# Down weights in longer runs, eight slots and another order of tiles, in a kernel that ends in 16 experts

## The chip, the cores and the metric

The kernel runs on one core of a Trainium2 chip. The metric is the time of one execution on the device in microseconds (us), a median over runs. Lower is better.

## What is computed

The program is three transformer layers over 256 tokens of width 1024, in float32. The first two have a mixer (a recurrence, two kinds of attention), a cross attention and a gated feed-forward part; the third has an adaptive modulation, a windowed attention with a gated branch, and a feed-forward part of 16 experts. Each expert takes the 32 tokens that score highest for it (cap = 2 x 256 / 16). The change is about the experts:

```
aff = softmax(h @ w_router);  gates, idx = top_k(aff.T, cap)      # 16 experts, 32 tokens each
xs  = h[idx]
hid = silu(xs @ w_gate[e]) * (xs @ w_up[e])     # w_gate, w_up: 16 x 1024 x 2816
out = (hid @ w_down[e]) * gates                 # w_down: 16 x 2816 x 1024
y   = zeros.at[idx].add(out);   x = x + gate2 * rms_norm(y)
```

The weights of one expert are 3 x 1024 x 2816 x 4 bytes = 34.60 MB (11.53 MB each of gate, up and down), those of all experts 553.6 MB. Each is read once.

## The kernel before

The first part of the program (mixers, cross attentions, feed-forward parts and the third layer up to its routing) runs out of a pool of tiles called `work`, whose first lines give every tag its place: the split activations `hH` and `hL`, `raw` (three weight buffers of 1 MB that SyncE fills), `wh` and `wl` (the weights split in two halves by ScalarE and VectorE), `gain`, `xg`, `dg`, `junk`, `mH` and `mL`, and small ones. `run_program` issues the loads of `raw` as buffers come free. The routing's constants and `mods` lie in another pool at the upper end.

`routing` ends that part: it norms the tokens, scores them, finds the 32 best per expert with VectorE, builds the selectors `sel` and gathers the tokens by matmul out of `mH` and `mL` into `xsT` (L1588 to L1594).

`experts` then frees `work` and takes the same memory for `e_pool`. `SLOTS_AT` is the order of its tiles in memory: a number is a slot for weights (5632 columns, 22,528 bytes a partition), a name is another tile. There are `E_BUFS` slots, used in turn. `loads` lists all pieces in their order: per expert four times a gate and an up piece (256 rows, two per partition, so that a partition's 22,528 bytes are contiguous in memory, and the piece is one block of 2.88 MB), then six down pieces. A down piece is two blocks of 256 rows (two rows per partition, 8192 bytes contiguous, 2 MB in all), the sixth one block. `feed` issues pieces on SyncE's queue (L1641 down, L1644 gate and up) as far as slots go; `take` feeds one more whenever TensorE's code comes to a piece. A piece waits for everything that used the memory of its slot: the first seven for tiles of `work` and of the routing, all later ones for the matmuls on the slot's piece before. SyncE issues in order, so one that waits holds back those behind it.

Per expert, TensorE multiplies the 32 tokens (`xsT`, 32 columns) by gate and up pieces (L1670): seven matmuls per 128 rows and kind, four of 512 and three of 256 columns, each into its 32 partitions of `pg` and `pu`. ScalarE and VectorE make `hid` of them (L1675 to L1677), TensorE turns it by six transposes, ScalarE and VectorE copy the result to `hT` (L1684, L1688). Then come the down matmuls (L1698) into `pd`, ScalarE's copies to `ds` (L1700, L1701), four matmuls with the gates' selector `sT` into `po` (L1705), which put the 32 tokens in their places, and VectorE's additions to `y` in SBUF (L1710). At the end `y` is normed (squares on ScalarE, L1717; the gain on VectorE, L1718; the root on GpSimd, L1722 and L1723), added to `x` and stored.

## Time and profile before

| | us |
|---|---|
| median of three runs | 2364.9 (2364.6 to 2369.95) |
| the profiled execution | 2368.78 |
| its span | 2367.0 |
| first matmul of the experts | 1085.83 |
| last matmul record's start of the down weights, and its length | 2347.58, 5.32 |

A page shows one profiled execution: busy times of the engines, the span in 40 slices (59.2 us each) with the share of the 16 DMA engines and the bytes that they moved, and the chain of waits that ended last. The table of stretches gives the same for any stretch: busy time of each engine, the granted clock of TensorE as a share of 2.4 GHz, the mean busy share of the DMA engines (a little over 1 where transfers overlap) and GB/s. A timeline lists instructions in order of time: start, length, engine, line, operation, tiles, and in brackets the idle time before it and what ended that.

### The profile page before, as it was taken

What the parts mean: (1) busy time and instruction counts of PE and PEld (TensorE: products, weight loads), DVE (VectorE), ACT (ScalarE), POOL (GpSimd) and SP (SyncE); (2) the same over time, 40 slices, a digit from 0 to 9 for tenths busy, and PEclk for the clock granted to TensorE, in tenths of its full rate; (3) what the DMA queues carried; (4) which work ended last, traced back from release to release, by engine and by line L of the source; (5) the groups of instructions that cost most, each with busy time, mean ns of one, the idle gap of its engine ahead of it and who ended that gap; (6) DMA issues with size and microseconds to landing.
All of it is one profiled execution on the core that took longest, in us unless ns stands there. A gap on an engine that the chain in (4) does not pass through costs nothing.

```text
span 2367.0 us, 29153 instructions
## 1 busy us (share of the span) xinstructions
PE 1844.4 (78%) x12660; PEld 1169.9 (49%) x12660; DVE 743.7 (31%) x1099; ACT 539.7 (23%) x866; POOL 54.4 (2%) x96
## 2 busy tenths in 40 slices
PE   7999999999989999987666666665666656666665
PEld 7889899989878888973111111111111111111211
DVE  5775555567656555652000000000000000000001
ACT  4554444445534333531000000000000000000000
POOL 0010000000000000010000000000000000000000
PEclk9999999999999999978888778888778897887788
DMA  7345465553559886539999999999999999999996
GB/s 219 125 147 183 160 195 179 161 155 127 195 178 301 281 279 195 203 154 384 428 428 425 423 429 425 425 425 428 425 425 427 428 424 423 429 426 424 425 428 282
DMA packets 202320, 747.06 MB, mean 316 GB/s; under 512 B 17712, under 2 KB 148416, under 8 KB 163408
## 3 DMA queue, kind: packets, MB, share of 16 engines
q1 hardware_dynamic: 199600, 744.39, 80.0%
q8 instruction: 99, 1.62, 0.3%
q10 hardware_dynamic: 2592, 0.81, 0.2%
q14 instruction: 29, 0.24, 0.0%
HBM read 743.99 MB, written 1.05 MB: 315 GB/s over the span
## 4 chain that ended last, share of the span: by engine, by line
DMA 50%; PE 40%; DVE 5%; ACT 2%; POOL 1%; issue 1%; SPq 0%; ACTq 0%; POOLq 0%; DVEq 0%
DMA ed<-in_w_down_dram 23%; DMA eu<-in_w_up_dram 22%; DMA eg<-in_w_gate_dram 4%; PE pu L1670 3%; PE pd L1698 2%; PE fu L249 2%; PE fu L251 2%; PE fu L250 2%; PE fg L249 2%; PE fg L251 2%; PE fg L250 2%; PE facc L251 2%; PE facc L250 2%; PE facc L249 2%; DVE wl L207 1%
## 5 line engine op out<-in xcount | busy, mean ns | idle before, releaser
L1670 PE MATMUL pu<-eu,xsT 128*32 128x512 f32 (+1 forms) x1792 | 274.8, 728 | 180.7 <-DMA eu<-in_w_up_dram 180.7
L207 DVE TENSOR_TENSOR wl<-raw,wh 128x1024 fp32r<-128x1024 f32 (+1 forms) x284 | 341.6, 1216 | 226.7 <-ACT wh L206 226.1
L1698 PE MATMUL pd<-ed,hT 128*32 128x512 f32 x1408 | 230.3, 742 | 146.9 <-DMA ed<-in_w_down_dram 143.4
L206 ACT CAST wh<-raw 128x1024 fp32r<-128x1024 f32 (+1 forms) x284 | 292.2, 1043 | 224.5 <-PE fg L250 44.1
L1670 PE MATMUL pg<-eg,xsT 128*32 128x512 f32 (+1 forms) x1792 | 235.0, 636 | 112.7 <-DMA eg<-in_w_gate_dram 112.7
L1670 PEld LDWEIGHTS pu<-eu,xsT 128*32 128x32 f32 x1792 | 78.6, 143 | 370.9 <-DMA eu<-in_w_up_dram 214.4
L1676 DVE SCALAR_TENSOR_TENSOR hid<-hid,pg 128x512 f32<-128x512 f32 (+1 forms) x32 | 17.6, 549 | 693.2 <-ACT hid L1675 693.2
L1670 PEld LDWEIGHTS pg<-eg,xsT 128*32 128x32 f32 x1792 | 71.2, 129 | 282.2 <-DMA eg<-in_w_gate_dram 152.9
L1698 PEld LDWEIGHTS pd<-ed,hT 128*32 128x32 f32 x1408 | 48.7, 125 | 316.3 <-DMA ed<-in_w_down_dram 171.8
L1675 ACT ACTIVATE hid<-pg 128x512 f32<-128x512 f32 (+1 forms) x32 | 15.6, 489 | 755.8 <-PE pg L1670 743.7
L1710 DVE TENSOR_TENSOR y<-y,po 128x512 f32<-128x512 f32 x60 | 41.2, 687 | 374.3 <-PE po L1705 374.3
L249 PE MATMUL fu<-hH,wh 128*128 128x256 f32 x352 | 100.4, 285 | 0.0
L251 PE MATMUL fu<-hH,wl 128*128 128x256 f32 x352 | 100.3, 285 | 0.0
L250 PE MATMUL fu<-hL,wh 128*128 128x256 f32 x352 | 100.2, 285 | 0.0
L249 PE MATMUL fg<-hH,wh 128*128 128x256 f32 x352 | 99.6, 283 | 0.0
L250 PE MATMUL fg<-hL,wh 128*128 128x256 f32 x352 | 99.5, 283 | 0.0
L251 PE MATMUL fg<-hH,wl 128*128 128x256 f32 x352 | 99.5, 283 | 0.0
L1700 ACT COPY ds<-pd 128x512 f32<-128x512 f32 x16 | 9.4, 586 | 362.0 <-PE pd L1698 362.0
L251 PE MATMUL facc<-wh,dL 128*128 128x512 f32 x176 | 69.3, 393 | 0.0
L250 PE MATMUL facc<-wl,dH 128*128 128x512 f32 x176 | 68.9, 391 | 0.0
L249 PE MATMUL facc<-wh,dH 128*128 128x512 f32 x176 | 68.6, 390 | 0.0
L250 PEld LDWEIGHTS fu<-hL,wh 128*128 128x128 f32 x352 | 67.9, 193 | 0.0
(566 smaller groups left out, 3208.9 us busy)
## 6 DMA issues: line engine op xcount, KB each, us to landing
eg<-in_w_gate_dram SPq DMA_DIRECT2D x64, 2816.0 KB, 36.4
eu<-in_w_up_dram SPq DMA_DIRECT2D x64, 2816.0 KB, 37.3
ed<-in_w_down_dram SPq DMA_DIRECT2D x80, 2048.0 KB, 37.5
raw<-in_w_in_dram SPq DMA_DIRECT2D x31, 1024.0 KB, 5.6
adw<-in_w_ada_dram SPq DMA_DIRECT2D x24, 1024.0 KB, 8.5
raw<-in_w_gate_dram SPq DMA_DIRECT2D x22, 1024.0 KB, 5.4
raw<-in_w_up_dram SPq DMA_DIRECT2D x22, 1024.0 KB, 5.2
raw<-in_w_down_dram SPq DMA_DIRECT2D x22, 1024.0 KB, 4.9
```

The source lines that it names most:

```text
L206: nc.scalar.copy(h, v)
L207: nc.vector.tensor_tensor(l, v, h.bitcast(F32), op=OP.subtract)
L249: nc.tensor.matmul(o, aH, bH, start=first, stop=False)
L250: nc.tensor.matmul(o, aH, bL, start=False, stop=False)
L251: nc.tensor.matmul(o, aL, bH, start=False, stop=last)
L1670: nc.tensor.matmul(o, B["xsT"][:, k, 32 * e:32 * e + 32], w[:, a, d, :], start=k == 0, stop=k == KC - 1)
L1675: nc.scalar.activation(d, g, AF.Tanh, scale=0.5)
L1676: nc.vector.scalar_tensor_tensor(d, d, 1.0, g, op0=OP.add, op1=OP.mult)
L1698: nc.tensor.matmul(pd[n][32 * j:32 * j + 32, :], hT[:, 2 * (d // 4) + c % 2, s:s + 32], w[:, (c % 4) * D + n * 512:(c % 4) * D + n * 512 + ...
L1700: nc.scalar.copy(ds_[:, :512], pd[0])
L1710: nc.vector.tensor_tensor(yb, yb, po, op=OP.add)
```

## The change

Down weights come in four pieces per expert, each 22,528 contiguous bytes per partition: partition p holds rows 22p to 22p + 21 (90,112 bytes), and piece i is the i-th quarter of that. A piece is five and a half rows, 11 half rows of 512 columns. The last piece of all is cut in three (3072, 1536 and 1024 columns). So every expert has 12 pieces of 2.88 MB where it had eight of 2.88 MB and six of 2 or 1 MB.

So that the rows 22p + j lie on partition p, the features of `hid` are taken by quarters of 704: quarter q on partitions 32q and on, in 512 columns (`pg`, `pu`) and 192 more (`pr`, one PSUM bank for both kinds), eight matmuls per 128 rows and kind. VectorE's 32x32 transpose over `hid`, read with a step of 22, makes `hT` in one instruction. The second half of `pd` shares the bank of `pr`.

The experts' sums stay in four PSUM banks `y00` to `y11` over all experts. At the end they are squared out of PSUM, and the gain goes to a tile `yg` in a weight slot. The sum of squares is added on VectorE. `rows16` of the routing has a tile of its own. The space kept for DMA descriptors in SBUF is set to 512 bytes, the tags of `work` stand in another order with three gaps, and there are eight slots in the order of `SLOTS_AT`.

```
-E_BUFS = 7
-SLOTS_AT = [1, 5, 3, 4, 6, "y", "hid", "hT", "ds", "sT", "fs", 0, 2]
+E_BUFS = 8
+SLOTS_AT = [1, 2, 4, 5, 6, 7, 0, 3, "hid", "hT", "ds", "sT", "fs"]
...
+    tile_(work, (P, 48), "gap0")
     hH = tile_(work, (P, KC, S), "hH", F32R)
     hL = tile_(work, (P, KC, S), "hL", F32R)
-    for tag, n, dt, bufs in (("gain", D, F32, 2), ("dg", P, F32, 2), ("raw", 2048, F32, RAW_BUFS), ("wh", 1024, F32R, HALVES), ("wl", 1024, F32R, HALVES),
-                             ("junk", D, BF16, 1), ("tiny1", 1, F32, 8), ("xg", D, F32, 3), ("tiny8", 8, F32, 6), ("tiny2", 2, F32, 6), ("tiny16", 16, F32, 2),
-                             ("mH", 2048, F32, 1), ("mL", 2048, F32, 1)):
+    tile_(work, (P, 16), "gap1")
+    for tag, n, dt, bufs in (("raw", 2048, F32, RAW_BUFS), ("wh", 1024, F32R, HALVES), ("wl", 1024, F32R, HALVES), ("gap2", 320, F32, 1),
+                             ("gain", D, F32, 2), ("dg", P, F32, 2), ("xg", D, F32, 3), ("junk", D, BF16, 1), ("mH", 2048, F32, 1), ("mL", 2048, F32, 1),
+                             ("tiny1", 1, F32, 8), ("tiny8", 8, F32, 6), ("tiny2", 2, F32, 6), ("tiny16", 16, F32, 2)):
...
-        sc = work.tile([16, 512], F32, name="rows16", tag="junk", bufs=1)
+        sc = tile_(p, (16, 512), "rows16")
...
-                    nw = min(2, NW - 2 * k)
-                    to = t[:, :nw * 2 * D].rearrange("p (d c n) -> p d c n", d=nw, c=2)
-                    src = I["w_down_2"][0, e, 512 * k:512 * k + 256 * nw, :].rearrange("(d p c) n -> p d c n", p=P, c=2)
-                    if st["n"] == len(loads) - 1:
-                        for n0 in range(0, D, 512):
-                            nc.sync.dma_start(to[:, 0, :, n0:n0 + 512], src[:, 0, :, n0:n0 + 512])
-                    else:
-                        nc.sync.dma_start(to.rearrange("p d c n -> p d (c n)"), src.rearrange("p d c n -> p d (c n)"))
+                    src = I["w_down_2"][0, e].rearrange("(p j) n -> p (j n)", p=P)[:, 2 * D_FF * k:2 * D_FF * (k + 1)]
+                    cut = (0, 3072, 4608, 2 * D_FF) if st["n"] == len(loads) - 1 else (0, 2 * D_FF)
+                    for c0, c1 in zip(cut, cut[1:]):
+                        nc.sync.dma_start(t[:, c0:c1], src[:, c0:c1])
...
-                        for b in range(2):
-                            for j in range(4 - b):
-                                d = slice(j, j + 5, 4) if b == 0 else slice(j + 8, j + 9)
-                                o = pg[n][32 * j:32 * j + 32, b, :512 - 256 * b].rearrange("p (d f) -> p d f", f=256)
-                                nc.tensor.matmul(o, B["xsT"][:, k, 32 * e:32 * e + 32], w[:, a, d, :], start=k == 0, stop=k == KC - 1)
+                        xs = B["xsT"][:, k, 32 * e:32 * e + 32]
+                        for q in range(4):
+                            nc.tensor.matmul(pg[n][32 * q:32 * q + 32, :], xs, w[:, a, q, 0:512], start=k == 0, stop=k == KC - 1)
+                        for q in range(4):
+                            nc.tensor.matmul(rest[n][32 * q:32 * q + 32, :], xs, w[:, a, q, 512:], start=k == 0 and n == "g", stop=k == KC - 1 and n == "u")
...
-            hT = e_pool.tile([P, 6, P], F32, name=f"hT{e}", tag="hT", bufs=1)
-            hv = hid.rearrange("p d (q a) -> p d a q", a=2)
-            pt = pq.tile([P, 4, P], F32, name=f"pt{e}a", tag="pm", bufs=2)
-            for m in range(4):
-                nc.tensor.transpose(pt[:, m, :], hv[:, m // 2, m % 2, :], ident)
-            nc.scalar.copy(hT[:, 0:4, :], pt)
...
+            hT = e_pool.tile([P, NJ, 32], F32, name=f"hT{e}", tag="hT", bufs=1)
+            nc.vector.transpose(hT, hid.rearrange("p (a j) -> p j a", j=NJ))
...
-            for q in range((NW + 1) // 2):
-                w = take("d", e, q)
+            for i in range(4):
+                w = take("d", e, i)
                 for n in range(2):
-                    for c in range(4 * q, min(4 * q + 4, 2 * NW)):
-                        d, j = c // 2, c % 4
-                        s = 32 * (d % 4)
-                        nc.tensor.matmul(pd[n][32 * j:32 * j + 32, :], hT[:, 2 * (d // 4) + c % 2, s:s + 32], ...
+                    for h in range(11 * i, 11 * i + 11):
+                        j = h // 2
+                        if h % 2 == n:
+                            nc.tensor.matmul(pd[n][32 * (j % 4):32 * (j % 4) + 32, :], hT[:, j, :], w[:, 512 * (h - 11 * i):512 * (h - 11 * i) + 512], start=j < 4, stop=j + 4 >= NJ)
             nc.scalar.copy(ds_[:, :512], pd[0])
-            nc.scalar.copy(ds_[:, 512:], pd[1])
+            if e < NE - 1:
+                nc.scalar.copy(ds_[:, 512:], pd[1])
+            else:
+                nc.vector.tensor_copy(ds_[:, 512:], pd[1])
             for n in range(2):
                 for t in range(2):
-                    po = pq.tile([P, 512], F32, name=f"po{e}_{t}{n}", tag="pm", bufs=2)
-                    nc.tensor.matmul(po, sT[:, t * P:(t + 1) * P], ds_[:, n * 512:(n + 1) * 512], start=True, stop=True)
...
-                        nc.vector.tensor_tensor(yb, yb, po, op=OP.add)
+                    nc.tensor.matmul(y[t][n], sT[:, t * P:(t + 1) * P], ds_[:, n * 512:(n + 1) * 512], start=e == 0, stop=e == NE - 1)
...
-            nc.gpsimd.tensor_scalar(ss, ss, fs[:, 2 * t + 1:2 * t + 2], EPS, op0=OP.add, op1=OP.add)
+            nc.vector.tensor_scalar(ss, ss, fs[:, 2 * t + 1:2 * t + 2], EPS, op0=OP.add, op1=OP.add)
...
-    nc = _bacc.Bacc("TRN2", target_bir_lowering=False, num_devices=1)
+    nc = _bacc.Bacc("TRN2", target_bir_lowering=False, num_devices=1, dynamic_dma_scratch_size=512)
```

Where instructions moved, and what they wait for: SyncE's queue around the first pieces of the experts. `DMAHW0` to `DMAHW7` are the semaphores of transfers, the other names those of engines, which stand for the last use of the memory under the slot; a row without waits goes right behind the one before it. Before:

```order
L1644 DMA eg0_0_10493<-in_w_gate_2_dram 128x5632 [waits DMAHW0_49,DMAHW2_49,DVE_49,PE_49]
L1644 DMA eu0_0_10495<-in_w_up_2_dram 128x5632 [waits PE_49]
L1644 DMA eg0_1_10497<-in_w_gate_2_dram 128x5632 [waits DMAHW2_49,DVE_49,PE_49]
L1644 DMA eu0_1_10499<-in_w_up_2_dram 128x5632 [waits DMAHW4_49,DMAHW5_49,DVE_49,PE_49]
L1644 DMA eg0_2_10501<-in_w_gate_2_dram 128x5632
L1644 DMA eu0_2_10503<-in_w_up_2_dram 128x5632 [waits DMAHW6_49,PE_49]
L1644 DMA eg0_3_10505<-in_w_gate_2_dram 128x5632 [waits PE_49,Pool_49]
L1649 DMA iota_10282<-in_k_iota_dram 128x256 [waits DMAHW7_49]
L1644 DMA eu0_3_10524<-in_w_up_2_dram 128x5632 [waits DMAHW0_49,PE_49]
L1641 DMA ed0_0_10540<-in_w_down_2_dram 128x2x2048 [waits DMAHW1_49,PE_49]
```

After:

```order
L1644 DMA eg0_0_10500<-in_w_gate_2_dram 128x5632 [waits DMAHW0_49,DMAHW2_49,DVE_49,PE_49]
L1644 DMA eu0_0_10502<-in_w_up_2_dram 128x5632 [waits PE_49]
L1644 DMA eg0_1_10504<-in_w_gate_2_dram 128x5632 [waits DMAHW5_49,DMAHW4_49,DMAHW6_49,DMAHW2_49,DVE_49]
L1644 DMA eu0_1_10506<-in_w_up_2_dram 128x5632 [waits PE_49]
L1644 DMA eg0_2_10508<-in_w_gate_2_dram 128x5632 [waits DVE_49,PE_49]
L1644 DMA eu0_2_10510<-in_w_up_2_dram 128x5632
L1644 DMA eg0_3_10512<-in_w_gate_2_dram 128x5632 [waits PE_49,Pool_49]
L1644 DMA eu0_3_10514<-in_w_up_2_dram 128x5632 [waits DMAHW7_49,DVE_49,Activation_49]
L1649 DMA iota_10285<-in_k_iota_dram 128x256 [waits DMAHW0_49]
L1641 DMA ed0_0_10536<-in_w_down_2_dram 128x5632 [waits DMAHW1_49,PE_49]
```

The eighth piece, `eu0_3`, stood behind the small table `iota` and waited for TensorE (its matmuls on `eg0_0`); now it stands ahead of it and waits for VectorE and ScalarE (`xsT`). The first down piece waits for those matmuls instead. The third, fourth and fifth pieces changed what they wait for, and the sixth waits for nothing of its own.

VectorE's queue in the last expert and behind it, to the end (`hid15` is the expert's hidden part, `fs` the sums of squares, `x_66` the residual). Before:

```order
L1676 SCALAR_TENSOR_TENSOR hid15_13982<-hid15_13982,pg15_13851 128x512
L1677 SCALAR_TENSOR_TENSOR hid15_13982<-hid15_13982,pu15_13852 128x512
L1676 SCALAR_TENSOR_TENSOR hid15_13982<-hid15_13982,pg15_13851 96x256
L1677 SCALAR_TENSOR_TENSOR hid15_13982<-hid15_13982,pu15_13852 96x256
L1688 COPY hT15_13989<-pt15b_13996 128x2x96
L1690 TENSOR_SCALAR sT15_14000<-iota_10282,idxT_10283,gateT_10284 128x256
L1710 TENSOR_TENSOR y_10485<-y_10485,po15_00_14051 128x512
L1710 TENSOR_TENSOR y_10485<-y_10485,po15_10_14054 128x512
L1710 TENSOR_TENSOR y_10485<-y_10485,po15_01_14057 128x512
L1710 TENSOR_TENSOR y_10485<-y_10485,po15_11_14060 128x512
L1718 TENSOR_TENSOR y_10485<-y_10485,mod5_6812 128x512 x4
L1724 SCALAR_TENSOR_TENSOR x_66<-y_10485,fs_10490,x_66 128x1024 x2
```

After:

```order
L1678 SCALAR_TENSOR_TENSOR hid15_13943<-hid15_13943,pr15_13802 128x192
L1681 STREAM_TRANSPOSE hT15_13950<-hid15_13943 128x704
L1683 TENSOR_SCALAR sT15_13952<-iota_10285,idxT_10286,gateT_10287 128x256
L1697 COPY ds15_14000<-pd15_1_13955 128x512
L1708 TENSOR_TENSOR yg_14008<-y00_10496,mod5_6815 128x512
L1708 TENSOR_TENSOR yg_14008<-y10_10498,mod5_6815 128x512
L1708 TENSOR_TENSOR yg_14008<-y01_10497,mod5_6815 128x512
L1708 TENSOR_TENSOR yg_14008<-y11_10499,mod5_6815 128x512
L1711 TENSOR_SCALAR fs_10495<-fs_10495 128x1
L1713 SCALAR_TENSOR_TENSOR x_66<-yg_14008,fs_10495,x_66 128x1024
L1711 TENSOR_SCALAR fs_10495<-fs_10495 128x1
L1713 SCALAR_TENSOR_TENSOR x_66<-yg_14008,fs_10495,x_66 128x1024
```

The transpose stands where a copy of TensorE's transposes stood; the four additions are gone, a copy of `pd` came, and the second sum of squares stands behind the first output pass.

## Rows read from the trace of the kernel before

**Rows 1.** The page: the span, its 40 slices, the chain that ended last.

```profile
span 2367.0 us, 29153 instructions
...
GB/s 219 125 147 183 160 195 179 161 155 127 195 178 301 281 279 195 203 154 384 428 428 425 423 429 425 425 425 428 425 425 427 428 424 423 429 426 424 425 428 282
...
DMA ed<-in_w_down_dram 23%; DMA eu<-in_w_up_dram 22%; DMA eg<-in_w_gate_dram 4%; PE pu L1670 3%; PE pd L1698 2%; PE fu L249 2%; PE fu L251 2%; PE fu L250 2%; PE fg L249 2%; PE fg L251 2%; PE fg L250 2%; PE facc L251 2%; PE facc L250 2%; PE facc L249 2%; DVE wl L207 1%
```

**Rows 2.** Table of stretches, one in the expert stage (columns in its first row).

```profile
core 0: us, PE busy (x) PEld busy (x) DVE busy (x) ACT busy (x) POOL busy (x), PEclk, DMA share, GB/s
1200.00:1300.00 100.00, 70.26 (x402) 19.47 (x402) 8.30 (x14) 3.91 (x7) 0.00 (x0) 0.78 1.01 427
```

**Rows 3.** Table of stretches, the last gap ahead of the stream.

```profile
1086.00:1088.00 2.00, 2.00 (x22) 0.65 (x17) 0.73 (x1) 0.00 (x0) 0.00 (x0) 1.00 0.04 9
1088.00:1089.00 1.00, 1.00 (x17) 0.52 (x14) 0.00 (x0) 0.00 (x0) 0.00 (x0) 1.00 0.00 0
```

**Rows 4.** Timeline of SyncE's queue, four of the first eight pieces' issues.

```profile
997.10 0.34 SPq L1644 DMA_DIRECT2D eg<-in_w_gate_dram  x1
...
1044.66 0.33 SPq L1644 DMA_DIRECT2D eg<-in_w_gate_dram  x1
...
1075.27 0.33 SPq L1644 DMA_DIRECT2D eg<-in_w_gate_dram  x1
...
1088.66 0.33 SPq L1644 DMA_DIRECT2D eu<-in_w_up_dram  x1
```

**Rows 5.** Table of stretches, the end of the stream.

```profile
2342.00:2344.00 2.00, 1.51 (x16) 0.42 (x16) 0.00 (x0) 0.00 (x0) 0.00 (x0) 1.00 0.58 239
...
2346.00:2348.00 2.00, 0.42 (x4) 0.19 (x8) 0.00 (x0) 0.00 (x0) 0.00 (x0) 0.98 0.50 190
2348.00:2350.00 2.00, 2.00 (x16) 0.74 (x10) 0.00 (x0) 0.00 (x0) 0.00 (x0) 0.50 0.25 92
```

**Rows 6.** Stretches of gate and up loads alone, each followed by one of down.

```profile
1128.00:1176.00 48.00, 30.91 (x195) 9.00 (x195) 2.77 (x4) 1.04 (x2) 0.00 (x0) 0.80 1.00 428
1181.00:1203.00 22.00, 13.54 (x98) 3.75 (x90) 2.11 (x5) 0.59 (x1) 0.00 (x0) 0.89 1.01 420
...
2189.00:2230.00 41.00, 27.19 (x172) 8.43 (x173) 2.75 (x4) 0.59 (x1) 0.00 (x0) 0.81 1.00 429
2242.00:2257.00 15.00, 9.56 (x70) 2.98 (x67) 2.11 (x5) 0.59 (x1) 0.00 (x0) 0.84 1.01 421
```

**Rows 7.** The page's DMA issues: count, KB each, median us from issue to landing.

```profile
ed<-in_w_down_dram SPq DMA_DIRECT2D x80, 2048.0 KB, 37.5
...
raw<-in_w_gate_dram SPq DMA_DIRECT2D x22, 1024.0 KB, 5.4
...
raw<-in_w_down_dram SPq DMA_DIRECT2D x22, 1024.0 KB, 4.9
```

**Rows 8.** Timeline of TensorE and VectorE where the experts begin.

```profile
1085.83 2.56 PE L1670 MATMUL pg<-eg,xsT 128*32 128x512 f32 x25
...
1085.92 0.81 DVE L1592 TENSOR_SCALAR xsT<-pg,s 128x512 f32<-128x512 f32 x1 [1.03 <-PE pg L1589]
```

**Rows 9.** Timeline between up and down products of the second expert.

```profile
1184.99 0.69 DVE L1677 SCALAR_TENSOR_TENSOR hid<-hid,pu 128x512 f32<-128x512 f32 x1 [5.43 <-PE pu L1670]
...
1187.21 1.92 PE L1698 MATMUL pd<-ed,hT 128*32 128x512 f32 x16 [0.22 <-ACT hT L1684]
```

**Rows 10.** Timeline of the end, from the last down products on.

```profile
2347.58 5.32 PE L1698 MATMUL pd<-ed,hT 128*32 128x512 f32 x24 [3.17 <-DMA ed<-in_w_down_dram]
...
2352.83 3.95 PE L1705 MATMUL po<-ds,sT 128*128 128x512 f32 x8
...
2356.82 0.69 DVE L1710 TENSOR_TENSOR y<-y,po 128x512 f32<-128x512 f32 x1 [0.17 <-PE po L1705]
...
2357.58 1.22 POOL L1722 TENSOR_SCALAR fs<-fs 128x1 f32<-128x1 f32 x1 [1285.88 <-ACT fj L1717]
...
2361.88 1.28 DVE L1724 SCALAR_TENSOR_TENSOR x<-y,fs,x 128x1024 f32<-128x1024 f32 x1 [0.77 <-POOL fs L1723]
```

More of the change, by code (lines that the diff above doesn't have):

```diff
@@ L1597, in tile_kernel @@
     NE = 16
-    NW = D_FF // 256
+    NQ = D_FF // 4
+    NJ = D_FF // P
     def experts():
@@ L1612, in experts @@
             else:
-                shape = dict(y=(P, 2, D), hid=(P, 3, 256), hT=(P, 6, P), sT=(P, S), ds=(P, D), fs=(P, P))[nm]
+                shape = dict(hid=(P, NQ), hT=(P, NJ, 32), sT=(P, S), ds=(P, D), fs=(P, 4))[nm]
                 one[nm] = e_pool.tile(list(shape), F32, name=nm, tag=nm, bufs=2 if nm == "sT" else 1)
-        y = one["y"]
+        y = [[pq.tile([P, 512], F32, name=f"y{t}{n}", tag=f"y{t}{n}", bufs=1) for n in range(2)] for t in range(2)]
         loads = []
@@ L1622, in experts @@
                 loads.append(("u", e, i))
-            for q in range((NW + 1) // 2):
-                loads.append(("d", e, q))
+            for i in range(4):
+                loads.append(("d", e, i))
         got = {}
@@ L1686, in experts @@
-            for a in range(2):
-                nc.tensor.transpose(pt[:, a, 0:96], hv[0:96, 2, a, :], ident[0:96, 0:96])
-            nc.vector.tensor_copy(hT[:, 4:6, 0:96], pt[:, 0:2, 0:96])
+            hT = e_pool.tile([P, NJ, 32], F32, name=f"hT{e}", tag="hT", bufs=1)
+            nc.vector.transpose(hT, hid.rearrange("p (a j) -> p j a", j=NJ))
             sT = e_pool.tile([P, S], F32, name=f"sT{e}", tag="sT", bufs=2)
             nc.vector.tensor_scalar(sT, B["iota"], B["idxT"][:, e:e + 1], B["gateT"][:, e:e + 1], op0=OP.is_equal, op1=OP.mult)
-            pd = [pq.tile([P, 512], F32, name=f"pd{e}_{n}", tag=f"pd{n}", bufs=1) for n in range(2)]
@@ L1692, in experts @@
-            for q in range((NW + 1) // 2):
-                w = take("d", e, q)
+            pd = [pq.tile([P, 512], F32, name=f"pd{e}_{n}", tag=("pd", "pr")[n], bufs=1) for n in range(2)]
+            for i in range(4):
+                w = take("d", e, i)
                 for n in range(2):
-                    for c in range(4 * q, min(4 * q + 4, 2 * NW)):
-                        d, j = c // 2, c % 4
-                        s = 32 * (d % 4)
-                        nc.tensor.matmul(pd[n][32 * j:32 * j + 32, :], hT[:, 2 * (d // 4) + c % 2, s:s + 32], w[:, (c % 4) * D + n * 512:(c % 4) * D + n * 512 + 512], start=c < 4, stop=c + 4 >= 2 * NW)
+                    for h in range(11 * i, 11 * i + 11):
+                        j = h // 2
+                        if h % 2 == n:
+                            nc.tensor.matmul(pd[n][32 * (j % 4):32 * (j % 4) + 32, :], hT[:, j, :], w[:, 512 * (h - 11 * i):512 * (h - 11 * i) + 512], start=j < 4, stop=j + 4 >= NJ)
@@ L1719, in experts @@
         for t in range(2):
[L1720 removed]
             ss = fs[:, 2 * t:2 * t + 1]
[L1722 removed]
+            nc.vector.tensor_scalar(ss, ss, fs[:, 2 * t + 1:2 * t + 2], EPS, op0=OP.add, op1=OP.add)
             nc.gpsimd.tensor_tensor(ss, ss, mhalf[:, 0:1], op=OP.pow)
[L1724 removed]
+            nc.vector.scalar_tensor_tensor(x[:, t, :], yg[:, t, :], ss, x[:, t, :], op0=OP.mult, op1=OP.add)
```

29 lines of the change are left out of this document (11 added, 18 removed).

## The prediction

> **What bounds the kernel now.** I read the page first, then the stage table, then the stretches in which one kind of weight is loaded, then the two ends of the stream. [rows 1] shows two kernels in one: over the first 18 of 40 slices the DMA engines move 125 to 301 GB/s; from the 20th on they move 423 to 429 without a break. The chain that ended last agrees: down and up weights alone are 45% of it. In the expert stage the DMA share is 1.01 with TensorE busy 70 of 100 us [rows 2], and its granted clock (0.78, so now 2.4 and now 1.2 GHz) doesn't matter as long as it stays ahead. So the time is: when the stream of expert weights begins without a gap, how many bytes it then has to move, at which rate, and what follows its last byte. A faster TensorE, VectorE or ScalarE in between is worth nothing.
>
> The 16 experts have 16 x 34.60 MB. Before the gap, seven pieces of 2.88 MB are loaded; the DMA engines then stand still until the eighth is issued at 1088.66 [rows 3, 4], and stop at about 2349.5 [rows 5]. 533.5 MB in some 1259 us.
>
> **Part 1: down weights in runs of 22,528 bytes.** This is the main term. In the trace the two kinds of load follow each other, and seven pairs of stretches hold one kind alone: gate and up (runs of 22,528 bytes) 428, 428, 429, 430, 429, 429, 429 GB/s, down (runs of 8192 bytes) 420, 419, 421, 421, 420, 419, 421; the first and the last pair stand in [rows 6]. Means: 428.9 and 420.1. An expert's down weights are 11.53 MB: 11.53/420.1 = 27.45 us before, 11.53/428.9 = 26.89 after, 0.56 us per expert, 16 of them: **9.0 us**. Nothing hides or absorbs it: the share is 1.01 throughout, so a byte moved faster ends the stream earlier.
>
> There is a second, smaller part. From 2342 to 2349 the share is 0.5 [rows 5]: half of the engines have done their part some 8 us before the others, which set the end. The lag can grow by bytes (then it stays 8 us) or by runs. The stream after the gap has 15,488 long and 22,528 short runs before, 23,680 long ones after, 0.62 of the number; by runs the lag falls to 5 us, half of which the means above already hold: 0 or 1.5 us more.  I take 1.5, since a lag by bytes would need half of the engines to be slower in themselves, which no row shows, and keep 0 for the range: **10.5 us**.
>
> The Trainium skill (DMA: Bandwidth & Descriptors, "Why small descriptors are slow") gives a fixed 3 cycles per packet beside 32 bytes a cycle. As an estimate from that page of the Trainium skill, 259 cycles per 8192 bytes against 707 per 22,528 make down loads 0.74% faster, 3.3 us in all instead of 9.0; the rows show 2.1%, and by the measured stretches I go.
>
> What the trace doesn't show is a long run out of rows that lie apart: gate and up pieces are one block of 2.88 MB, down pieces were blocks of 1 MB, the new ones take 22,528 bytes out of every 90,112. The nearest rows are two 1 MB loads of the first stage, rows apart in 1 KB runs (gate, 5.4 us to land) and a block in 4 KB runs (down, 4.9 us) [rows 7]. That is at most 10% for spacing and short runs together, so the cost of spacing lies between 0 and 10% of 440 us. I take 0, since the runs are as long as those of gate and up; the rest is a rival.
>
> **Part 2: eight slots, other places.** [rows 4] gives the issues of the first pieces: 997.10 the first, 1044.66 the third, 1075.27 the seventh, each waiting for tiles of the routing stage that lie under its slot. In the new order pieces 3 to 7 come earlier (the third waits for the split of a weight on VectorE, the fourth for what the third waited for, the sixth comes with the fifth, the seventh no longer waits for the lists at 1075). But this fills idle time that costs nothing: seven pieces are in before 1088 either way. Only the eighth piece counts. Before, it waits for TensorE to be done with the first piece. After, its slot lies under the routing's halves and selectors, free when the last of xsT is written: 1085.92 + 0.81 = 1086.73 [rows 8]. It is issued 1.9 us earlier. The ninth piece waits for TensorE's first piece as the eighth did, 1.9 us later, while a piece takes 6.7 us to move, so the stream has no gap behind it. The small table (128 KB, 0.3 us) now moves within the stream instead of in the gap. **1.6 us.** Later a deeper queue gives nothing: a piece already waits 37 us behind others [rows 7], and the share leaves nothing to fill.
>
> **Part 3: the hidden steps.** Per expert: 16 narrower matmuls for 14 per piece; one VectorE transpose of 704 columns in place of six TensorE transposes and two copies; the sums of the experts stay in PSUM, four VectorE additions fewer. Now 2.2 us pass between the last up product's multiply and the first down matmul [rows 9]. The transpose isn't in the trace; from below it is free of the old copies (-2 us), from above I give it four times the 0.69 us of a 512-column VectorE pass, 3 us. Cost at the end: nothing, because six to seven pieces are queued behind (37 us). If a stall passed 37 us per expert, the cover would be gone. At the last expert four down pieces, 27 us, still lie between. TensorE needs about 2.6 us for a gate or up piece at granted clock 1.0, 2.4 GHz [rows 8], and at most twice that at 1.2; a new down piece has 11 matmuls for 8, at most 22 x 0.22 = 4.9 us [rows 10], under 6.7. The smaller scratch space costs nothing: every DMA of the kernel is issued from SyncE or ScalarE. The routing's little table in a tile of its own removes a wait that doesn't show (VectorE waits there for TensorE): 0.
>
> **Part 4: after the last byte.** Before: last byte at about 2349.5, pd done at 2347.58 + 5.32 = 2352.90, the four output products until 2356.8, the last addition until 2357.5, the end of VectorE's last pass at 2363.16 [rows 10]: 13.7 us. After: the last cut is 0.5 MB, and its matmul of the first half stands ahead of six of the second: 7 matmuls, 14 records of 0.12 [rows 9] to 0.22 us [rows 10], 1.7 to 3.1, with up to 1 us from byte to matmul: 2.2 to 3.6 against 3.4 now. Four output products, now without waits: 3.5 for 3.95. The last addition (0.69) goes; a square and a multiplication per quarter now go one after the other on the same PSUM bank, since the multiplication waits for ScalarE. The sum of squares goes from GpSimd (1.22 us) to VectorE (some 0.2), but the second stands behind the first output pass. In total I count 12.7, from 11.8 to 14: **1.0 us**, between 1.9 gained and 0.3 lost.
>
> **Sum.** 10.5 + 1.6 + 1.0 = 13.1 us. The profiled execution took 2368.8 us (span 2367.0 and 1.8 around it), so it would take 2355.7; it lies 3.9 above the median of the three runs, 2364.9, by which I forecast 2364.9 - 13.1 = 2351.8, rounded to **2352 us**. With the bounds (stream 9.0 to 12, start 1.3 to 2, tail -0.3 to 1.9) the gain is 10 to 16: 2349 to 2355; with runs that differ by some 5 us, 2346 to 2358. A measurement of this kernel tells about 0.3%, 7.1 us, from no change.
>
> **The rivals.**
> *Spaced runs gain nothing* (0.14): down loads stay at 420 GB/s because rows apart cost what long runs gain. Then 1.6 + 1.0 = 2.6 are left: 2362, within 0.3%. For it: no row shows this pattern; against: the kernel's column loads differ by 0.5 us with runs a quarter as long.
> *Spaced runs are slower* (0.04): the mechanism is that the 16 engines read at addresses 90,112 bytes apart and meet in the memory. It decides from where a down piece takes longer than now by 2.6/64 = 0.04 us, at 418 GB/s, and the kernel is slower by 0.3% at 411. At the bound of [rows 7], 10% on 16 x 27.45, it costs 44 us instead of gaining 10.5: 2364.9 + 44 - 2.6 = 2406. Against it: the engines aren't at a limit of the memory that the trace shows, since two kinds of load differ by run length alone.
> *A pitch that halves the rate* (0.01): the same mechanism at its hardest, 16 x 27.45 us once more, some 2800.
> [...]
> *TensorE or VectorE becomes the bound in the experts* (0.03): needs 20 us more per expert, of the 81.6 that its 34.60 MB take at 424 GB/s; every 1 us beyond costs 16: 2364 to 2400. Against it: the sum in part 3.
> *More than forecast* (0.06): the lag of half the engines goes altogether, 5 us more, or the stage before starts the stream earlier: 2345.
>
> **How the numbers follow.** The forecast has 0.72. The range 2344 to 2361 holds it, the better case and a good part of the first rival, in which the rate lies between; the slower cases, 0.08, and the rest of the first rival stay out. Faster by over 0.3% (below 2357.8): 0.72 + 0.06 and a little of the first rival, 0.80. Within 0.3%: the rest of it and a part of the TensorE case, 0.13. Slower: 0.07.
>
> **What would show it.** Part 1: stretches of down loads alone at 429 GB/s instead of 420; if they read 420 or less, the term is wrong. The lag: a share of 0.5 for 5 us instead of 8 at the end. Part 2: the eighth piece issued at about 1086.8, the ninth near 1088.5, no empty microsecond from 1089 on. Part 3: a transpose under 3 us, TensorE waiting for DMA between pieces in every expert. Part 4: under 13 us from the last byte to VectorE's last pass. The prediction is wrong if the stage up to 1085 us moves by more than 3 us, or if the share in the experts falls below 1.0.

## The result and the profile after

The changed kernel takes 2338.15 us (median of 4 runs, 2334.9 to 2338.86); the kernel before, run beside it, 2367.07 us (4 runs, 2364.6 to 2369.95). The ratio is 0.9875, 95% interval 0.9858 to 0.9892. The forecast was 2352 us with a range of 2344 to 2361. The kernel gained 29 us where 13 were forecast, so the time lies below the range.

The profiled executions took 2368.78 and 2338.86 us, a difference of 30 us. The page of the changed kernel, as [rows 1] of before (its second line is the memory traffic of 40 equal slices, its third the DMA issues of the down weights as in [rows 7], with count, KB each and median us to landing):

```profile
span 2336.4 us, 29792 instructions
...
GB/s 218 131 145 188 153 206 186 161 162 137 192 186 293 284 284 207 195 247 360 429 428 429 429 428 430 429 427 430 428 429 429 429 429 429 430 428 429 429 428 280
...
ed<-in_w_down_dram SPq DMA_DIRECT2D x63, 2816.0 KB, 50.5
```

The stream now holds 427 to 430 GB/s where it held 423 to 429: that is the part that was forecast. The other part stands where the experts begin. The timeline (start us, duration us, engine, line, operation, out<-in, count, and in brackets the idle time before it and what ended it), and after it SyncE's queue:

```profile
1065.21 1.07 PE L1670 MATMUL pg<-eg,xsT 128*32 128x512 f32 x8
...
1065.32 0.81 DVE L1595 TENSOR_SCALAR xsT<-pg,s 128x512 f32<-128x512 f32 x1 [1.04 <-PE pg L1592]
```

```profile
981.99 0.34 SPq L1644 DMA_DIRECT2D eg<-in_w_gate_dram  x1
...
1051.21 0.33 SPq L1644 DMA_DIRECT2D eg<-in_w_gate_dram  x1
1066.19 0.33 SPq L1644 DMA_DIRECT2D eu<-in_w_up_dram  x1
...
1067.84 7.43 SPq L1641 DMA_DIRECT2D ed<-in_w_down_dram  x4
```

The first matmul of the experts starts at 1065.21, in [rows 8] at 1085.83: **20.6 us of the 30 are gained before the experts begin**, in a stage in which the diff changes hardly an instruction. The prediction held that stage to be unchanged.

Where in the stage? Compared matmul by matmul, the lead grows wherever TensorE is the bound: 1.1 us at 112 us, 8 at 454, 12 at 717, 15 at 967. I took equal stretches of 10 us inside a gate product of the first feed-forward part (fg: hH and hL moved through wh and wl). The columns are the stretch, its length, busy time and instructions of PE, PEld, DVE, ACT and POOL, the granted clock, the DMA share and GB/s. The kernel before, then the changed one:

```profile
312.00:322.00 10.00, 10.00 (x86) 10.00 (x85) 5.07 (x5) 4.43 (x5) 0.00 (x0) 1.00 0.64 211
329.00:339.00 10.00, 10.00 (x86) 10.00 (x85) 5.05 (x5) 4.45 (x5) 0.00 (x0) 1.00 0.65 211
```

```profile
309.00:319.00 10.00, 10.00 (x90) 10.00 (x89) 5.46 (x5) 4.49 (x5) 0.00 (x0) 1.00 0.67 211
325.50:335.50 10.00, 10.00 (x90) 10.00 (x89) 5.56 (x5) 4.38 (x5) 0.00 (x0) 1.00 0.63 211
```

TensorE is busy without a break in both, its granted clock is 1.00 (2.4 GHz) in both, the same transfers run, and yet 90 matmuls fit where 86 did (both counts include two or three that lie across an edge). From start to start, the 256-column fp32r matmuls of the stage that follow each other directly take 119.2 ns before and 115.0 after (some 4,600 pairs in each trace); fg alone 119.7 and 114.3. With 4,800 of them in the stage that is 20 us; the 512-column ones went from 228.2 to 229.3 ns, which costs 1 us. So the step of the matmul gives 19 us, of 20.6 measured.

That the two are so near is in part chance. Waits and all else take back some 7 us, and the stretches in which one of the two ran at 1.2 GHz give some 8: in the stage, the granted clock was 0.50 for 68 us in the trace of before and for 41 us in the one after. Most of the growth of the lead from 15 us at 967 to 20.6 stands in such stretches; one of before, then one of after at nearly the same work:

```profile
1020.00:1030.00 10.00, 8.64 (x41) 8.68 (x41) 8.34 (x12) 5.37 (x7) 0.81 (x2) 0.50 0.01 2
```

```profile
1000.00:1010.00 10.00, 6.66 (x54) 6.30 (x54) 7.42 (x12) 5.02 (x8) 1.28 (x2) 0.98 0.19 80
```

One trace of each kernel doesn't tell whether the change has a part in the clock.

What the diff changes for the fp32r matmuls is only where their operands lie in SBUF. Before, hH starts at byte 32,000 of each partition and the first wh at 82,176: a distance that is a multiple of 256. After, with `gap0` and `gap1`, they start at 16,320 and 57,344: a multiple of 256 and 64 more. The experiments ask whether that is the cause, and what the forecast parts are worth one by one.

### The profile page after: what moved, and what is told of

Read it like the earlier page. It is cut to its first block, busy times and chain, and to the rows that moved or that the text cites. A ratio compares the mean times of both kernels' runs of the same rounds, so it can differ in the third digit from the quotient of the medians.

```text
span 2336.4 us, 29792 instructions
## 1 busy us (share of the span) xinstructions
PE 1820.1 (78%) x13076; PEld 1150.0 (49%) x13076; DVE 722.7 (31%) x1038; ACT 528.8 (23%) x849; POOL 51.0 (2%) x94
## 4 chain that ended last, share of the span: by engine, by line
DMA 46%; PE 41%; DVE 6%; ACT 2%; another core or an unknown queue 1%; issue 1%; POOL 1%; SPq 1%; ACTq 0%; POOLq 0%; DVEq 0%
DMA eg<-in_w_gate_dram 17%; DMA eu<-in_w_up_dram 15%; DMA ed<-in_w_down_dram 12%; PE pd L1691 3%; PE fu L252 2%; PE fu L254 2%; PE fu L253 2%; PE fg L252 2%; PE fg L254 2%; PE fg L253 2%; PE pu L1670 2%; PE facc L254 2%; PE facc L253 2%; PE facc L252 2%; PE pg L1670 1%
## 5 line engine op out<-in xcount | busy, mean ns | idle before, releaser
L1691 PE MATMUL pd<-ed,hT 128*32 128x512 f32 x1408 | 279.1, 731 | 146.1 <-DMA ed<-in_w_down_dram 103.0
L1670 PE MATMUL pu<-eu,xsT 128*32 128x512 f32 x1024 | 201.7, 871 | 170.1 <-DMA eu<-in_w_up_dram 170.1
L1670 PE MATMUL pg<-eg,xsT 128*32 128x512 f32 x1024 | 189.9, 823 | 123.5 <-DMA eg<-in_w_gate_dram 123.5
L1691 PEld LDWEIGHTS pd<-ed,hT 128*32 128x32 f32 x1408 | 65.9, 124 | 352.1 <-issue 153.8
L1670 PEld LDWEIGHTS pu<-eu,xsT 128*32 128x32 f32 x1024 | 35.4, 141 | 210.4 <-DMA eu<-in_w_up_dram 198.3
L1670 PEld LDWEIGHTS pg<-eg,xsT 128*32 128x32 f32 x1024 | 33.8, 135 | 168.3 <-DMA eg<-in_w_gate_dram 156.5
L1672 PEld LDWEIGHTS pr<-eu,xsT 128*32 128x32 f32 x1024 | 43.8, 148 | 129.7 <-issue 129.7
L1672 PEld LDWEIGHTS pr<-eg,xsT 128*32 128x32 f32 x1024 | 41.8, 141 | 120.5 <-issue 120.5
L1672 PE MATMUL pr<-eu,xsT 128*32 128x192 f32 x1024 | 90.7, 436 | 0.0
L1672 PE MATMUL pr<-eg,xsT 128*32 128x192 f32 x1024 | 86.0, 416 | 0.0
```

Of the source, the lines that this page charges most:

```text
L1670: nc.tensor.matmul(pg[n][32 * q:32 * q + 32, :], xs, w[:, a, q, 0:512], start=k == 0, stop=k == KC - 1)
L1672: nc.tensor.matmul(rest[n][32 * q:32 * q + 32, :], xs, w[:, a, q, 512:], start=k == 0 and n == "g", stop=k == KC - 1 and n == "u")
L1691: nc.tensor.matmul(pd[n][32 * (j % 4):32 * (j % 4) + 32, :], hT[:, j, :], w[:, 512 * (h - 11 * i):512 * (h - 11 * i) + 512], start=j < 4, ...
```

## The experiments

Theory A: the distance between the two operands of a matmul, counted within 256 bytes, sets its step. Rival D: the new sequence of tiles as a whole, or the small DMA scratch, gave the time. Ratios are to the kernel before, run beside each.

**1. The matmul by itself.** A kernel with nothing but groups of 48 matmuls on two tiles that lie alike, each group with the moved operand, the weights or both shifted; once upwards (x) and once downwards (y).

```
+ nc.tensor.matmul(o[:, :cols], W[:, so + s * P:so + s * P + P], M[:, mo + k * cols:mo + k * cols + cols], ...)
```

> The disputed cost by itself: groups of 48 matmuls of fp32r, 128 rows of weights by 256 moved columns (wide: 512), with nothing else running; the moved operand (mov), the weights (sta) or both (both) start 0 to 480 bytes further in steps of 32 (letters a to p), each group twice (x upwards, y downwards). All else of the model is left out. Theory A (where the two operands lie against each other in SBUF sets the step of a matmul): at full clock mova, every group of both, and movi if only the distance within 256 bytes counts, take about 120 ns a matmul; movc and movg (64 and 192 bytes apart) 113 to 116 ns; sta reads as mov. Rival B (the operand that lies 64 bytes off is quicker by itself, whatever the other does): both falls with mov. Rival C (placement is nothing to TensorE; what fell was contention with the other engines or with transfers): all groups within 1 ns.

Its timeline; a group starts where the one ahead of it has issued its 48, so the difference of two starts over 48 is the step:

```profile
22.05 5.92 PE L102 MATMUL movxa<-M,W 128*128 128x256 f32 x48
27.80 5.82 PE L102 MATMUL movxb<-M,W 128*128 128x256 f32 x48
33.46 5.82 PE L102 MATMUL movxc<-M,W 128*128 128x256 f32 x48
39.12 5.91 PE L102 MATMUL movxd<-M,W 128*128 128x256 f32 x48
...
204.02 5.91 PE L102 MATMUL bothxc<-M,W 128*128 128x256 f32 x48
209.76 5.91 PE L102 MATMUL bothxd<-M,W 128*128 128x256 f32 x48
...
284.48 11.05 PE L102 MATMUL widexa<-M,W 128*128 128x512 f32 x48
295.37 11.37 PE L102 MATMUL widexb<-M,W 128*128 128x512 f32 x48
306.58 11.16 PE L102 MATMUL widexc<-M,W 128*128 128x512 f32 x48
317.57 11.37 PE L102 MATMUL widexd<-M,W 128*128 128x512 f32 x48
...
896.33 5.61 PE L102 MATMUL movyc<-M,W 128*128 128x256 f32 x48
901.77 5.78 PE L102 MATMUL movyb<-M,W 128*128 128x256 f32 x48
```

Operands that lie alike: (27.80 - 22.05)/48 = 119.8 ns. The moved one 64 bytes further: (39.12 - 33.46)/48 = 117.9 on the way up and (901.77 - 896.33)/48 = 113.3 on the way down. Both 64 bytes further (bothxc): 119.6 again. The weights 64 bytes further, as in the kernel's fg: 113.8 and 113.6. The pattern repeats after 256 bytes about as well as the two rounds agree (320 reads as 64), 128 bytes give 118.6, and every group of both lies between 119.5 and 120.0. So it is the distance that counts; rivals B and C are out, since nothing else ran. With 512 columns it is the other way round: alike 10.89/48 = 226.9 ns, 64 bytes apart 229.0, 32 or 96 apart 233 to 234. That the same distance gives 113.3 or 117.9 I had not expected: of the 16 groups 64 or 192 bytes apart (also counted within 256), seven step at 113.3 to 114.0 ns and nine at 117.8 to 117.9, both movg groups among the nine, where 113 to 116 was expected. The runs don't say what decides between the two.

**2. One shift in the kernel before.** Six small tiles, 192 bytes together, go ahead of the raw weights and their halves.

```
-    for tag, n, dt, bufs in (("gain", D, F32, 2), ... ("tiny8", 8, F32, 6), ...
+    for tag, n, dt, bufs in (("tiny8", 8, F32, 6), ("gain", D, F32, 2), ...
```

> The kernel before with one edit: six small tiles (192 bytes together) are reserved ahead of the gains, raw weights and their halves instead of behind them, so these lie 192 bytes further, and hH and hL stay. No instruction moves. Theory A: 256-column matmuls of the stage before the experts fall from 120 to 113 to 116 ns, the first matmul of the experts comes 16 to 22 us earlier (1064 to 1070 us, before 1085.8), the whole 16 to 22 us faster. Rival D (the new sequence of tiles as a whole, what overlaps what, or the small DMA scratch gave the 20 us): within 3 us of the kernel before.

2361.25 us (ratio 0.9983, 0.9972 to 0.9995). First matmul of the experts at 1077.4, so 8.4 us earlier and not the 16 to 22 expected. The step: 117.4 ns in the mean; fg and fu fell to 117.2 to 118.3, but kp and vp, whose moved or stationary operand is memH or memL, rose to 119.7, because wh now lies alike with these, and many 512-column ones (mo, cacc) rose from 227 to 228 to 233. The theory holds and its size was wrong: a shift helps one pair of tiles and harms another.

**3. The changed kernel without its 64 bytes.**

```
-    tile_(work, (P, 16), "gap1")
-    ... ("gap2", 320, F32, 1),
+    ... ("gap2", 336, F32, 1),
```

> The changed kernel without its second gap: its 16 numbers go to the third, so that the raw weights and their halves lie 64 bytes nearer and hH, hL, wh and wl all lie alike within 512 bytes, as they did before the change; all behind them stays. Theory A: the first matmul of the experts at 1082 to 1087 us, total 2354 to 2360 us (the changed kernel 2338), that is, only what the stream and the tail brought is left. Rival D: 2338 within 3 us, the first matmul near 1065.

2360.39 us (ratio 0.9974, 0.9964 to 0.9984). The first matmul of the experts, and the same stretches of fg:

```profile
1087.65 1.06 PE L1669 MATMUL pg<-eg,xsT 128*32 128x512 f32 x8
...
314.50:324.50 10.00, 10.00 (x85) 10.00 (x85) 4.98 (x5) 4.51 (x5) 0.00 (x0) 1.00 0.63 211
331.50:341.50 10.00, 10.00 (x85) 10.00 (x84) 5.00 (x5) 4.49 (x5) 0.00 (x0) 1.00 0.60 211
```

85 again, 119.8 ns in the mean. **An unused tile of 64 bytes is worth 22 us of the change's 29.** Rival D, as far as it means the sequence of tiles without that gap, is out. It isn't quite the layout of before: memH now lies alike with wh too, so that kp and vp step at 119.7 and 119.8 ns (115.1 and 117.2 before) and the 512-column mo and cacc at 233.4 (227.5). By the steps that is some 5 us more than in the kernel before, and so only 6 us of what the experts gained are left in the total.

**4. The small scratch alone**, in the kernel before.

```
-    nc = _bacc.Bacc("TRN2", target_bir_lowering=False, num_devices=1)
+    nc = _bacc.Bacc("TRN2", target_bir_lowering=False, num_devices=1, dynamic_dma_scratch_size=512)
```

> The kernel before with the small DMA scratch alone: every tile lies 15,872 bytes lower, a multiple of 512, and nothing else changes. Theory A: within 2 us of the kernel before, first matmul of the experts 1084 to 1088 us. Rival D, if the scratch is the part that helped: 15 to 20 us faster.

2367.3 us, ratio 1.0002 (0.9991 to 1.0013), first matmul of the experts at 1083.7. It gives nothing.

**5. Twice the gap** in the changed kernel.

```
-    tile_(work, (P, 16), "gap1")
+    tile_(work, (P, 32), "gap1")
-    ... ("gap2", 320, F32, 1),
+    ... ("gap2", 304, F32, 1),
```

> The changed kernel with its second gap doubled to 32 numbers (the third 16 smaller): wh and wl lie 128 bytes from hH and hL, counted within 256, in place of 64. The bare groups give 118.6 ns at 128 bytes. Theory A: fg and fu 118 to 119 ns, facc near 233, the first matmul of the experts 15 to 20 us later than in the changed kernel, 1079 to 1085 us; total 2353 to 2358 us. Rival H (any gap does, it only has to keep the two apart): 1065 us and 2338 as now.

2358.69 us (ratio 0.9967, 0.9956 to 0.9977); the step is 119.0 ns, facc 232.4, the first matmul of the experts at 1088.46. The direction is as expected, the stage 3 us worse than the range. So not every gap helps.

**6. The kernel before with the right distance: three tries.** First 320 bytes of small tiles ahead of the raw weights (320 is 256 and 64).

```
+    for tag, n, dt, bufs in (("tiny8", 8, F32, 6), ("tiny16", 16, F32, 2), ("gain", D, F32, 2), ...
```

> The kernel before with one edit, the other sign of the one that moved the raw weights and halves 192 bytes on (it gained 8.4 us at the first matmul of the experts, its 256-column matmuls at 117.4 ns): two groups of small tiles, 320 bytes, are reserved ahead of them, so that wh and wl lie 64 bytes beyond hH and hL, counted within 256, as in the changed kernel. Theory A, with the sizes of the bare groups (64 bytes: 113.4 or 117.9 ns; none: 119.9): fg, fu, cq at 113 to 116 ns, the first matmul of the experts at 1065 to 1073 us, total 12 to 21 us under the kernel before. Rival D (the new sequence of tiles is needed as well): no more than the 8 us of the other shift.

The step fell to 115.7 ns and the first matmul of the experts came at 1072.99, 12.8 us earlier, as expected. But the total is 2364.53 us (ratio 0.998, 0.997 to 0.9989): from that matmul to the end it now takes 1292.1 us in place of 1281.2. The sixth piece of the experts was issued at 1073.9 instead of 1065.1, after the first matmul. The small tiles that I moved now lie under that piece's slot; it waited 30.2 us for VectorE, until xsT was done. Second, an unused tile behind hL, with the small scratch to make room:

```
     hL = tile_(work, (P, KC, S), "hL", F32R)
+    tile_(work, (P, 16), "gap")
```

> The kernel before with two edits: the small DMA scratch (alone it was 1.0002 of the kernel before), and an unused tile of 16 numbers behind hL, so that wh and wl lie 64 bytes beyond hH and hL, counted within 256, and every tile in use keeps its order. Theory A: fg, fu and cq at 113 to 116 ns as in the changed kernel, the first matmul of the experts at 1061 to 1068 us (1083.7 with the scratch alone), the loads of the experts' first seven pieces issued that much earlier too, and the total down by the same 16 to 22 us: 2344 to 2352 us. Rival D (the new sequence of tiles is needed): no more than the 8 us that the shift by 192 bytes gave.

fg reaches 91 in 10 us, the mean step 114.8 ns, xsT is done at 1068.24 (1084.62 with the scratch alone) — and the kernel takes 2393.73 us (ratio 1.0114, 1.0095 to 1.0132). SyncE's waits (who, for whom: us in total, times, longest) and the timeline show why:

```profile
SPq L1645 <- DVE sel L1583: 84.0, 1, 84.0
```

```profile
1066.99 0.40 PE L1590 MATMUL pg<-sel,mL 128*128 128x512 f32 x1
1067.42 0.34 SPq L1645 DMA_DIRECT2D eg<-in_w_gate_dram  x1
...
1077.41 4.99 PE L1671 MATMUL pg<-eg,xsT 128*32 128x512 f32 x28 [10.02 <-DMA eg<-in_w_gate_dram]
```

All tiles behind the gap went up by 64 bytes, the experts' slots didn't. The first slot begins at byte 143,072, and sel now ends at 143,104: 32 bytes of overlap, and the first load waits for the last matmul that reads sel (the row of waits names the instruction that wrote it; the load follows the matmul of 1066.99 to 1067.39 by 0.03 us). The other six wait behind it in SyncE's queue. TensorE then waits 10 us for the first piece, and the seven pieces that used to move during routing move afterwards. Third, 64 unused bytes at the head of the experts' pool too, so that the slots go along:

```
         one = {}
+        tile_(e_pool, (P, 16), "egap")
```

> The kernel before with the small DMA scratch, the unused 64 bytes behind hL, and 64 unused bytes at the head of the experts' pool as well, so that the slots lie on the same tiles as before (without that, the first slot reached 32 bytes into the memory of mod2 and sel2, which routing reads last, and the loads began at 1067.4 us in place of 995.0). Theory A: 256-column matmuls near 115 ns, xsT done at 1063 to 1069 us as in the run without the second gap (1068.24), seven loads out before 1056 us, then the same 1281 us from the first matmul of the experts to the end as in the kernel before, so 2343 to 2351 us in all. Rival D (the new sequence of tiles is needed for the gain in the total): 2358 us or more.

2347.33 us, ratio 0.9913 (0.9897 to 0.993), and the first matmul of the experts at 1069.15. Its stretches of fg:

```profile
311.00:321.00 10.00, 10.00 (x90) 10.00 (x90) 5.43 (x5) 4.52 (x5) 0.00 (x0) 1.00 0.67 211
327.50:337.50 10.00, 10.00 (x90) 10.00 (x90) 5.53 (x5) 4.41 (x5) 0.00 (x0) 1.00 0.64 211
```

From the first matmul to the end 1279.5 us, nearly the 1281.2 of before. So unused bytes alone turn 2367.3 (the scratch alone) into 2347.3. Two details missed the expectation by little: xsT was done at 1070.0 and the seventh load issued at 1060.0. In its profiled execution this kernel reached the experts 4 us later than the changed kernel. Its steps are those of the changed kernel (114.9 and 229.3 ns in the mean), but its stage ran 68 us at a granted clock of 0.50 where the changed kernel's ran 41. Three profiled executions of kernels whose work ahead of the experts is the changed kernel's word for word reached them at 1061.6, 1062.6 and 1065.2, so differences of 3 to 4 us between single traces say nothing.

**7. Down weights in 8192-byte runs again**, in the changed kernel.

```
-                    cut = (0, 3072, 4608, 2 * D_FF) if st["n"] == len(loads) - 1 else (0, 2 * D_FF)
+                    cut = (0, 3072, 4608, 2 * D_FF) if st["n"] == len(loads) - 1 else (0, 2048, 4096, 2 * D_FF)
```

> The changed kernel with each down piece asked for by three DMAs of columns (8192, 8192 and 6144 bytes a row) in place of one of 22,528 bytes; same bytes, same slots, same matmuls. The prediction's rate (428.9 against 420.1 GB/s over 63 pieces): 8 to 9.5 us slower, 2346 to 2348 us, the down stretches at 420 to 421 GB/s, and half of the DMA engines still 8 to 10 us behind at the end. Rival E (the stream has one rate, set elsewhere, and the length of a run is nothing): within 2 us of 2338.

2348.99 us (ratio 0.9931, 0.9908 to 0.9953), 10.8 us slower where 8 to 9.5 were expected (two of its four runs took 2345 us, two 2353; the trace is of a 2345). From the first matmul of the experts to the end 1281.7 us for 1271.1. Down loads alone, then gate and up alone:

```profile
1156.00:1178.00 22.00, 16.43 (x94) 4.19 (x88) 3.48 (x5) 0.33 (x1) 0.00 (x0) 0.81 1.01 418
1185.00:1230.00 45.00, 27.93 (x204) 9.14 (x201) 0.00 (x0) 0.59 (x1) 0.00 (x0) 0.81 1.00 428
1237.00:1259.00 22.00, 16.51 (x96) 4.04 (x91) 3.48 (x5) 0.33 (x1) 0.00 (x0) 0.77 1.02 421
```

As [rows 6]; the changed kernel reads 428 to 433 in such stretches. Each piece is also three DMAs here in place of one, but [rows 6] has 420 with one DMA per down piece. The length of the run is worth some 10 us, and rival E is out.

**8. Seven slots.** A first run took the eighth tile out of the order altogether.

```
-E_BUFS = 8
-SLOTS_AT = [1, 2, 4, 5, 6, 7, 0, 3, "hid", "hT", "ds", "sT", "fs"]
+E_BUFS = 7
+SLOTS_AT = [1, 2, 4, 5, 6, 0, 3, "hid", "hT", "ds", "sT", "fs"]
```

> The changed kernel with seven slots for the experts' pieces instead of eight (the eighth slot's memory stays empty). The prediction's term: the eighth piece then waits for the first slot to come free, is issued about 1.6 us later, and the whole is 1 to 2 us slower, with the rate of the stream unchanged at 428 to 430 GB/s. Rival F (the deeper queue itself gives rate): 4 us slower or more. Rival G (the eighth slot is nothing): within 0.5 us.

2385.89 us (ratio 1.0074, 1.0056 to 1.0092), 48 us slower than with eight, and not because of the number: without it, slots 0 and 3 lie 22,528 bytes lower, and the first load waits until VectorE has written the last of xsT.

```profile
SPq L1644 <- DVE xsT L1595: 92.2, 1, 92.2
```

It tells nothing of the eighth slot, but once more what an overlap costs. The second run left the slot's memory empty where it was.

```
-E_BUFS = 8
+E_BUFS = 7
```

> The changed kernel with its eighth slot left empty where it lies, so that the first seven pieces use the same memory as in the changed kernel (the run with seven slots had moved them). The first seven loads are issued as now; the eighth waits for the first slot to come free. The prediction's term: it is issued some 1.6 us later, total 1 to 2 us slower than the changed kernel, 2339 to 2340 us, rate of the stream as now. Rival G: nothing, within 0.5 us. Rival F (the deeper queue gives rate): 4 us slower or more.

2341.03 us (ratio 0.99, 0.9883 to 0.9916). The eighth piece is issued 2.64 us behind the first matmul of the experts (1065.28 and 1062.64) where the changed kernel does it after 0.98; from that matmul to the end 1272.4 us for 1271.1. The eighth slot is worth 1.2 us in the trace, as the prediction's term has it; the medians differ by 2.9 us, with intervals that overlap.

**9. The 512-column matmuls as well**: 64 bytes more at the head of both feed-forward pools of the changed kernel.

```
             M["p"] = tc.alloc_tile_pool(name=f"ffn{l}", bufs=1, reuse_waits="tile")
+            tile_(M["p"], (P, 16), f"gap{l}")
```

> The changed kernel with 64 bytes more at the head of the pools of both feed-forward parts, so that dH and dL (stationary in facc's 512-column matmuls) lie alike with wh and wl within 256 bytes. The bare groups say that 512 columns go the other way than 256: alike 227 ns, 64 bytes apart 229, else 233. Theory A: facc from 229.8 to 232 down to 227 to 228 ns, some 530 matmuls, so 1 to 2.5 us off the first matmul of the experts (1065.2) and off the total. If only the bare groups behave so: no change within 1 us.

2338.23 us (ratio 0.9881, 0.9864 to 0.9899), the same as the changed kernel. facc did fall, from 230 to 232 down to 227.1 ns, as the bare groups say, which is 2 us; but fg and fu, whose operands did not move, step at 115.6 to 116.9 ns where they stepped at 114.2 to 115.8, which is about as much lost. The 1 to 2.5 us expected of the total didn't come. Different steps for one distance, as the bare groups showed, are in the kernel too. No run beat the changed kernel.

## Why the prediction was wrong, point by point

From the traces, with the stream's bytes after the first matmul of the experts (534.2 MB in both), its mean rate, and what its first and last 30 us lose against that rate:

| us | forecast | measured |
|---|---|---|
| stage ahead of the experts | 0 | -20.6 (1085.83 to 1065.21) |
| rate of the stream | -9.0 | -8.5 (425.9 to 428.9 GB/s, 1254.1 to 1245.6 us) |
| lag of half the engines at the end | -1.5 | +1.2 (4.83 to 6.07 lost) |
| start of the stream | -1.6 | -1.6 (4.85 to 3.21 lost) |
| from the last byte to the end | -1.0 | -1.1 (17.33 to 16.24) |
| sum | -13.1 | -30.6 |

The lines that were forecast gave 10.0 us of 13.1; the rest of the gain stands in the first line.

**The step that failed** is one that the sum took as given, that the stage ahead of the experts stays as it is; the prediction named it as its own condition ("if the stage up to 1085 us moves by more than 3 us"). Part 2 costed the order of tiles only through the slots that lie on them, part 3 the scratch at nothing (experiment 4 agrees), and no part gave the three gaps a cost or a gain. Experiments 1, 3 and 6 put the time there: 64 bytes between hL and the weights, 22 us in the one kernel and 20 in the other. The trace of before held the hint, though it could not be priced from there: fg and fu step at 119.7 to 119.9 ns, while other 256-column matmuls on the same engine at the same clock (kp on memH) step at 115. Two values for one shape were a question that I didn't ask. The rival "the stage before starts the stream earlier" shared a chance of 0.06 and a time of 2345 us with another and had no mechanism: so it doesn't count for the prediction that it points the right way.

**Part 1, the rate**: right. Down stretches went from 420 to 429; the long pitch costs nothing, a 22,528-byte packet takes 845 ns before and after (16,384 and 24,448 of them), and an 8192-byte packet 315. Rivals one to three fell with that.

**The lag**: wrong. I chose a lag by runs over a lag by bytes. The end of the changed kernel's stream:

```profile
2308.00:2310.00 2.00, 2.00 (x17) 0.54 (x12) 0.00 (x0) 0.00 (x0) 0.00 (x0) 1.00 1.00 416
2310.00:2312.00 2.00, 0.65 (x2) 0.00 (x0) 0.00 (x0) 0.00 (x0) 0.00 (x0) 1.00 0.51 214
...
2316.00:2318.00 2.00, 2.00 (x17) 0.55 (x10) 0.00 (x0) 0.00 (x0) 0.00 (x0) 0.75 0.43 173
2318.00:2320.00 2.00, 2.00 (x12) 0.40 (x5) 0.00 (x0) 0.00 (x0) 0.00 (x0) 1.00 0.14 56
```

The share falls to one half at 2310 and the last byte lands at 2320.1, 10 us later; [rows 5] showed about 8. With 8192-byte runs in the changed kernel the loss at the end is 6.5 us, so the number of runs doesn't make it. It is 4.8 to 5.6 us in the kernel before and its variants and 6.0 to 6.5 in all variants of the changed one; which of the remaining differences adds the 1.2 us stays open.

**Part 2, the start**: right in size and mechanism. The eighth piece was issued 0.98 us after TensorE's first matmul, before 2.83 ([rows 4, 8]); the ninth at 1067.84, as forecast relative to it. What the section didn't say is how near the cliff lies: with another overlap of slots and tiles the seven pieces ahead are lost, 27 us net in experiment 6 (46 against the same kernel with its slots moved along), 48 us in experiment 8.

**Part 3, the hidden steps**: right. VectorE's transpose takes 1.79 us, DMA is at 427 to 430 GB/s throughout.

**Part 4, the tail**: right in its sum, but by luck of the clock. The last cut, the output products, one square and multiplication, and the last pass:

```profile
2320.60 2.76 PE L1691 MATMUL pd<-ed,hT 128*32 128x512 f32 x14 [0.21 <-DMA ed<-in_w_down_dram]
...
2323.29 3.70 PE L1700 MATMUL y<-ds,sT 128*128 128x512 f32 x8
...
2327.81 0.69 DVE L1708 TENSOR_TENSOR yg<-y,mod 128x512 f32<-128x512 f32 x1 [0.17 <-ACT fj L1707]
2328.41 0.20 DVE L1711 TENSOR_SCALAR fs<-fs 128x1 f32<-128x1 f32 x1
...
2331.36 1.28 DVE L1713 SCALAR_TENSOR_TENSOR x<-yg,fs,x 128x1024 f32<-128x1024 f32 x1 [0.67 <-POOL fs L1712]
```

14 records in 2.76 us lie within the 1.7 to 3.1 of the forecast, the products take 3.70 (3.95 in [rows 10]), the sum of squares 0.20 on VectorE for 1.22 on GpSimd. But the forecast took the last down products of before as [rows 10] has them, 24 records in 5.32 us, and these ran at a granted clock of 0.50 ([rows 5], 2348 to 2350). In three variants of the kernel before (the three tries of experiment 6) they ran at 1.00; the third:

```profile
2330.91 3.63 PE L1700 MATMUL pd<-ed,hT 128*32 128x512 f32 x24 [1.70 <-DMA ed<-in_w_down_dram]
```

From the last byte to the end these three take 15.6 to 15.7 us, the changed kernel and its variants, at 1.00 as well, 16.2. At the same clock the new tail is some 0.6 us longer, which lies outside the part's bounds (1.9 gained to 0.3 lost). That also is why the third try takes 1279.5 us from its first expert matmul on, and not 1281.2.

## What to carry to other kernels

When a change moves tiles in SBUF, look where the two operands of the busiest matmuls lie against each other and what lies under each buffer that is loaded ahead: here 64 unused bytes were worth 20 us, and 32 bytes of overlap with a tile that is read late cost more than that. Before a gain of 1 us at the end of a kernel is put down to the change, compare the granted clock there. If one shape of matmul steps at two speeds in one trace at the same clock, ask why before taking the stage as given. A shift that helps one pair of tiles can harm another, so measure the whole stage and not one product.
